# Four blocks of a 31-tap convolution get set places behind the heads' projections on VectorE's queue

## The chip, the cores and the metric

The kernel runs on one core of a Trainium2 chip. The metric is the device time of one execution in microseconds; the kernel before takes 781.31 us (median of three runs, 781.28 to 781.71). The core has five engines with queues of their own, each worked through in order: TensorE (PE in the profile; its weight loads are listed as PEld), VectorE (DVE), ScalarE (ACT), GpSimd (POOL) and SyncE (SP), which issues most of the loads. An engine waits at the head of its queue until what its next instruction needs is there.

## What is computed

One layer of a decoder, for 512 positions of 1024 channels. A first half mixes two groups of channels that come from one input projection: four mLSTM heads of 256 channels, and a convolution group. A second half is a feed-forward network with a short convolution. Both are scaled by a modulation that a second input c gives. Cut to what the change touches:

```python
u = rms_norm(x, mix_pre_g) * (1.0 + sc1) + sh1
proj = u @ w_in
qk_raw, v, o_pre, gates, glu = jnp.split(proj, [2*D_ML, 3*D_ML, 4*D_ML, 4*D_ML + 2*H], axis=-1)

qk = jax.nn.silu(causal_dwconv(qk_raw, qk_conv_w, qk_conv_b))      # 4 taps
h = mlstm_chunkwise(q, k, v, igates, fgates)                       # 4 heads
h = rms_norm(h) * jax.nn.sigmoid(o_pre)

a, gt = jnp.split(glu, 2, axis=-1)
y = causal_dwconv(a * jax.nn.sigmoid(gt), cv_dw_w, cv_dw_b)        # 31 taps
y = jax.nn.silu(layer_norm(y, cv_ln_g, cv_ln_b))

mix = jnp.concatenate([h, y], axis=-1) @ w_out
x = x + g1 * rms_norm(mix, mix_post_g)
```

## The kernel before

Channels lie on the 128 partitions and the 512 positions along the free dimension, so the 1024 channels of the convolution group are eight tiles of 128 x 512, the blocks 0 to 7. Products on TensorE are made of three parts: each operand is split into a rounded high part (`hi`, a copy on ScalarE) and the rest (`lo`, a subtraction, mostly on GpSimd), and `mm3` (L186 to L190) adds high x high, high x low and low x high in one PSUM bank. The weights come through two raw buffers, loaded from SyncE's queue, and are split in `w_split` (L164).

The order of the stages on TensorE is: the projection of the convolution group (`glu`), v of head 0, then for each head six projections of 128 channels (two of q, two of k, two of the output gate o), its attention, and v of the next head; then the output projection, in which the convolution's result y is used as well, and the feed-forward half. `head_proj(h, i)` (L430) makes projection i of head h: 24 matmuls, and for q and k (`i < 4`) the short convolution `conv4` (L408): a start on ScalarE (L412), three taps on VectorE (L414) and a Silu on ScalarE (L415). `attention(h)` (L447) is a generator: its pieces are called between the projections of the next head (L705 to L731). At its end VectorE scales the head's rows (`hn`, L482) by a factor that GpSimd computes (L477 to L479), TensorE turns them (`hT`, L488), and VectorE and ScalarE gate and split them (L490 to L494). `make_E` (L531) makes the next head's decay factors: a product `Mb` (L533), a masked copy `Md` on VectorE (L535), and exponentials on ScalarE (L540, L542).

The long convolution is the loop at L646 over the eight blocks. In a block, ScalarE writes the first term into a PSUM bank (`cp`, L649; there are two such banks), ScalarE and GpSimd make five further taps in SBUF (L655, L657; the tiles of the pool `cvs`, four of them), and VectorE adds the other 25 taps, one instruction each, all into the same bank (L661): tap d covers 512 - d positions, so a block's taps run from 506 columns down to 482. Then ScalarE copies the bank out (L663), GpSimd adds the five side taps (L665), and running sums of the mean and the square over the blocks follow (L671 to L676). TensorE reads these sums in `norm_mean` (L682), late in the third turn of the head loop, and y is then normalised in `norm_rows` (L695).

SyncE and TensorE work in the order in which the code is written. The order on VectorE, ScalarE and GpSimd is made when the kernel is built, by a planner that goes through its own model of time and puts the ready instruction with the lowest priority number next on each engine's queue. The priority is a counter that rises with the code; work between `tc.cur_priority += LATER` and its reverse gets 100000 more, so the convolution's blocks fill the places that the heads' work leaves. An edge given by hand (`tc.add_manual_dep` with the class NoSync) tells the planner that one instruction must stand behind another on the same queue; it adds no wait on the chip.

Behind the last tap of the last block stand eight products of the modulation (`ada_block(i, last_tap)`, i from 16 to 23, L734): each is a load of 512 KB issued from ScalarE's queue (L153) into one of two buffers, and one instruction on VectorE (L155) with its accumulator read. Their result is needed for the first gains (L738).

Of the kernel before, what the change touches and what calls it, by code (L numbers as in the profile page):

```python
# [14 lines left out]
ALU = mybir.AluOpType  # L15
# [4 lines left out]
T = 512  # L20
KT = D // P
# [5 lines left out]
CK = 31  # L27
LATER = 100000
# [24 lines left out]
def decoder_layer(ctx, tc, w_glu0, x, c, adaT, vecs, w_glu, w_qko, w_v0, w_v, w_out, w_up, w_down, out):  # L53
    nc = tc.nc
    V, S, G, PE = nc.vector, nc.scalar, nc.gpsimd, nc.tensor
# [28 lines left out]
    def slot(name, dt=F32):  # L84
        return slots.tile([P, T], dt, tag="t", name=name)

    def mmbank(name):
        return psum.tile([P, T], F32, tag="mm", bufs=4, name=name)

    def atbank(name):  # L90
        return psum.tile([P, T], F32, tag="at", bufs=2, name=name)
# [5 lines left out]
    def cvbank(name):  # L97
        return cvpool[0].tile([P, T], F32, tag="cv", name=name)
# [30 lines left out]
    def vcol(name, i):  # L129
        a = VEC[name][0] + i  # L130
        return vec[:, a : a + 1]
# [15 lines left out]
    def ada_block(i, behind):  # L147

        if i % 6 < 4 and 24 <= i < 40:
            r = spare[0][:, 2 * (i % 6) : 2 * (i % 6) + 2, :].rearrange("p j t -> p (j t)")  # L150
        else:
            r = adas.tile([P, D], F32, tag="ada", name=f"ada_{i}")
        nc.scalar.dma_start(r, adaT[i // 2][:, (i % 2) * D : (i % 2 + 1) * D])  # L153
        junk = small.tile([P, D], BF16, tag="junk", bufs=1, name=f"junk_{i}")
        t = V.scalar_tensor_tensor(out=junk, in0=r, scalar=1.0, in1=cb, op0=ALU.mult, op1=ALU.mult, accum_out=mod[:, i : i + 1])  # L155
        tc.add_manual_dep(t.ins, behind.ins.name, mybir.DependencyInfo(mybir.DependencyClass.NoSync, mybir.DependencyReason.DATA),
                          reason="order on VectorE")

    def ada_done(a, b):
        V.tensor_tensor(out=mod[:, a:b], in0=mod[:, a:b], in1=vcols("ada_b", a, b - a), op=ALU.add)  # L160
# [84 lines left out]
    for tt in range(NT):  # L245
# [11 lines left out]
        if tt == NT - 1:  # L257
# [9 lines left out]
                    op0=ALU.add)  # L267
# [80 lines left out]
    cvx = [None] * KT  # L348
# [8 lines left out]
    def proj(ps, pieces, off):  # L357
        for k in range(KT):
            mm3(ps, blk(pieces, off + k), u[k], k == 0, k == KT - 1)
# [4 lines left out]
    for i in range(G0 // 2, KT):  # L364
        glu_weights(i)
        for half in range(2):
            ps = mmbank(f"glu{i}_{half}")
# [40 lines left out]
    def conv4(ps, i, name):  # L408

        t = slot(f"{name}c")  # L410
        w = lambda tap: vcol("qk_conv_w", tap * 16 + i)
        S.activation(t, ps, AF.Identity, bias=vcol("qk_conv_b", i), scale=w(3))  # L412
        for d in range(1, 4):
            V.scalar_tensor_tensor(out=t[:, d:], in0=ps[:, : T - d], scalar=w(3 - d), in1=t[:, d:], op0=ALU.mult, op1=ALU.add)  # L414
        S.activation(t, t, AF.Silu)  # L415
        return t

# [2 lines left out]
    hy = [None] * (2 * KT)  # L420

    heads = {}

    def head_load(h):
        pieces = []
        for part in range(3):
            pieces += w_load(w_qko[3 * h + part], f"wqko{h}_{part}")
        heads[h] = (pieces, [], [], [])

    def head_proj(h, i):  # L430

        pieces, qs, ks, so = heads[h]
        ps = mmbank(f"qko{h}_{i}")
        proj(ps, pieces, i * KT)
        e = 2 * h + i % 2
        if i < 2:
            qs.append(conv4(ps, e, f"q{h}_{i}"))
        elif i < 4:
            ks.append(conv4(ps, 8 + e, f"k{h}_{i}"))
        else:  # L440
            t = slot(f"so{h}_{i}")
            S.activation(t, ps, AF.Tanh, scale=0.5)
            so.append(t)

    last_lo = [None]

# [96 lines left out]
    head_load(0)  # L543
    for i in range(3):
        head_proj(0, i)

    fps = atbank("fcum")
    fv = fps[:, : NT * H].rearrange("p (t h) -> p t h", t=NT)
# [3 lines left out]
    V.tensor_copy(Fc, fv)  # L552
    V.tensor_tensor(out=ga, in0=gz[:, :, :H], in1=Fc, op=ALU.subtract)
    head_proj(0, 3)

    aps = atbank("aT")
# [5 lines left out]
    S.activation(Ms[:H, :], Mr, AF.Copy)  # L562
    V.tensor_tensor(out=Ms[LOW : LOW + H, :], in0=Mr, in1=Ms[:H, :].bitcast(F32), op=ALU.subtract)
    head_proj(0, 4)
    mps = atbank("mtok")
    mv = mps[:, : NT * H].rearrange("p (t h) -> p t h", t=NT)
# [38 lines left out]
    def cvtile(name):  # L605
        return cvs.tile([P, T], F32, tag="cvs", name=name)
# [31 lines left out]
            mm3(ps, (hy[k][0][:, tok(tt)], hy[k][1][:, tok(tt)]), wo[0][n % 4], n == 0, n == 2 * KT - 1)  # L638


    tc.cur_priority += LATER

    ys = [None] * KT
    ysum = const.tile([P, T], F32, name="ysum")
    ysq = const.tile([P, T], F32, name="ysq")
    for j in range(KT):  # L646
        cp = cvbank(f"cv{j}")
        w = lambda tap: cvw[:, tap * KT + j : tap * KT + j + 1]
        S.activation(cp, cvx[j], AF.Identity, bias=vcol("cv_dw_b", j), scale=w(CK - 1))  # L649
        side = None  # L650
        for d in range(1, SIDE + 1):
            t = cvs.tile([P, T], F32, tag="cvs", name=f"cs{j}_{d}")
            if d == 1:
                V.memset(t[:, :d], 0.0)
            S.activation(t[:, d:], cvx[j][:, : T - d], AF.Copy, scale=w(CK - 1 - d))  # L655
            if side is not None:
                G.tensor_tensor(out=side[:, d:], in0=side[:, d:], in1=t[:, d:], op=ALU.add)  # L657
            else:
                side = t
        for d in range(SIDE + 1, CK):  # L660
            last_tap = V.scalar_tensor_tensor(out=cp[:, d:], in0=cvx[j][:, : T - d], scalar=w(CK - 1 - d), in1=cp[:, d:], op0=ALU.mult, op1=ALU.add)  # L661
        y = cvx[j]
        S.activation(y, cp, AF.Copy)  # L663
        if side is not None:
            G.tensor_tensor(out=y, in0=y, in1=side, op=ALU.add)  # L665
        ys[j] = y

        if j:
            mean_of = ys[0] if j == 1 else ysum
            dl = cvtile(f"ydl{j}")  # L670
            V.scalar_tensor_tensor(out=dl, in0=mean_of, scalar=-1.0 / j, in1=y, op0=ALU.mult, op1=ALU.add)  # L671
            dst = ysq if j == 1 else dl
            S.activation(dst, dl, AF.Square, scale=(j / (j + 1.0)) ** 0.5)
            if j > 1:
                G.tensor_tensor(out=ysq, in0=ysq, in1=dl, op=ALU.add)
            G.tensor_tensor(out=ysum, in0=mean_of, in1=y, op=ALU.add)  # L676
    tc.cur_priority -= LATER

    def norm_mean():

# [51 lines left out]

    tc.cur_priority += LATER
    for i in range(16, 24):  # L734
        ada_block(i, last_tap)
    ada_done(16, 24)
    tc.cur_priority -= LATER
    gain(0, 16, "mix_post_g")  # L738
# [208 lines left out]
    for i in range(NF):  # L947
        if i < NE:
            pa, pg = early[i]
        else:  # L950
# [11 lines left out]
            for half in range(2):  # L962
                ps = mmbank(f"up{i}_{half}")
# [290 lines left out]
```

## Time and profile before

| what | value |
|---|---|
| median of three runs | 781.31 us |
| the profiled execution | 782.39 us |
| its span, first to last instruction | 780.6 us |
| granted TensorE clock, mean | 0.997 |
| busy: PE, DVE, ACT, POOL | 761.7, 591.3, 407.6, 383.9 us |
| convolution taps on VectorE (L661) | 200, 134.2 us, 54.4 to 232.6 us |
| the eight modulation products (L155) | 233.3 to 259.0 us |

Times are in microseconds from the start of the span. A row of the order of time gives the start, the duration, the engine, the line, the operation, the tiles (result <- operands) with their shapes, a count where rows of one kind are merged, and in square brackets the idle time of the engine before it and what ended it. ACTq is the issue of a transfer from ScalarE's queue. A row of the list of waits gives engine, tile and line that waited, what it waited for, the total time, the number of waits and the longest. The end of a matmul is modelled, and a busy TensorE is not one at its peak; its starts are what to go by.

### The profile page before, as it was taken

To read this page: it belongs to the slowest core of one execution; us is meant where nothing else is said; L and a number is where in the kernel's file an instruction comes from. 1 tells how busy PE (TensorE), PEld (TensorE's weight loads), DVE (VectorE), ACT (ScalarE), POOL (GpSimd) and SP (SyncE) were. 2 spreads that over 40 slices of the span, in tenths; PEclk is the share of its full clock that TensorE was granted. 3 is DMA by queue.
4 is the path that set the end of the run, shared out by engine and by line. 5 is a ranking of instruction groups with operands and counts; after the bars stand their busy time and mean duration, and the time that the engine had idled before them with its cause. 6 is when DMAs were issued, how large, how long until landed. Compare 5 with 4: busy or idle time off the path is not lost.

```text
span 780.6 us, 10572 instructions
## 1 busy us (share of the span) xinstructions
PE 761.7 (98%) x3683; PEld 635.0 (81%) x3683; DVE 591.3 (76%) x938; ACT 407.6 (52%) x766; POOL 383.9 (49%) x313
## 2 busy tenths in 40 slices
PE   7899999999999999999999999999999999999996
PEld 4678898878888888888878998888888888888884
DVE  7659999999998533555868799665556677699997
ACT  6576428668655554482244445444444444456762
POOL 3689759779778534334661446544454440000001
PEclk9999999999999999999999999999999999999998
DMA  8973313303117432424952763332333321777862
GB/s 297 325 293 126 107 58 108 135 29 109 55 57 248 154 103 86 143 105 144 391 196 103 242 230 136 129 108 93 124 115 128 116 101 61 260 273 235 299 241 108
DMA packets 35977, 124.28 MB, mean 159 GB/s; under 512 B 4146, under 2 KB 5586, under 8 KB 29908
## 3 DMA queue, kind: packets, MB, share of 16 engines
q1 hardware_dynamic: 24084, 95.15, 34.8%
q10 hardware_dynamic: 11840, 28.46, 10.2%
q8 instruction: 29, 0.48, 0.2%
q14 instruction: 24, 0.20, 0.1%
HBM read 112.17 MB, written 11.42 MB: 158 GB/s over the span
## 4 chain that ended last, share of the span: by engine, by line
PE 80%; DVE 10%; DMA 4%; issue 3%; POOL 1%; ACT 1%; ACTq 0%; POOLq 0%; DVEq 0%; SPq 0%
PE up L189 10%; PE up L188 10%; PE up L190 10%; DVE cv L661 5%; PE qko L188 4%; PE qko L189 4%; PE qko L190 4%; PE p L190 4%; PE p L189 4%; PE p L188 4%; PE glu L189 3%; PE glu L190 3%; PE glu L188 3%; DMA spare<-in_adaT 2%; PE o L466 2%
## 5 line engine op out<-in xcount | busy, mean ns | idle before, releaser
L661 DVE SCALAR_TENSOR_TENSOR cv<-gt,cvw,cv 128x506 f32<-128x506 f32 (+24 forms) x200 | 134.2, 728 | 0.4
L617 POOL TENSOR_TENSOR ro2r<-ro2t,mhalf 128x1 f32<-128x1 f32 x1 | 0.5, 538 | 120.7 <-DVE ro2t L615 120.7
L171 POOL TENSOR_TENSOR wup_1024l<-wup,wup_1024h 128x512 fp32r<-128x512 f32 x20 | 27.8, 1388 | 31.6 <-ACT wup_1024h L170 22.2
L171 POOL TENSOR_TENSOR wup_0l<-wup,wup_0h 128x512 fp32r<-128x512 f32 x20 | 27.8, 1388 | 29.4 <-ACT wup_0h L170 29.4
L657 POOL TENSOR_TENSOR cs<-cs,cs 128x510 f32<-128x510 f32 (+3 forms) x32 | 42.0, 1312 | 0.2
L171 POOL TENSOR_TENSOR wup_1536l<-wup,wup_1536h 128x512 fp32r<-128x512 f32 x20 | 28.4, 1422 | 27.2 <-ACT wup_1536h L170 27.2
L189 PE MATMUL up<-u2l,wup_0h 128*128 128x512 f32 (+1 forms) x100 | 36.5, 365 | 0.2 <-DVE u2l L830 0.2
L188 PE MATMUL up<-u2h,wup_0h 128*128 128x512 f32 (+1 forms) x100 | 36.5, 365 | 0.0
L188 PE MATMUL up<-u2h,wup_1024h 128*128 128x512 f32 (+1 forms) x100 | 36.4, 364 | 0.0
L190 PE MATMUL up<-u2h,wup_0l 128*128 128x512 f32 (+1 forms) x100 | 36.4, 364 | 0.0
L188 PE MATMUL up<-u2h,wup_512h 128*128 128x512 f32 (+1 forms) x100 | 36.4, 364 | 0.0
L189 PE MATMUL up<-u2l,wup_512h 128*128 128x512 f32 (+1 forms) x100 | 36.4, 364 | 0.0
L190 PE MATMUL up<-u2h,wup_512l 128*128 128x512 f32 (+1 forms) x100 | 36.4, 364 | 0.0
L188 PE MATMUL up<-u2h,wup_1536h 128*128 128x512 f32 (+1 forms) x100 | 36.4, 364 | 0.0
L189 PE MATMUL up<-u2l,wup_1536h 128*128 128x512 f32 (+1 forms) x100 | 36.4, 364 | 0.0
L190 PE MATMUL up<-u2h,wup_1536l 128*128 128x512 f32 (+1 forms) x100 | 36.4, 364 | 0.0
L190 PE MATMUL up<-u2h,wup_1024l 128*128 128x512 f32 (+1 forms) x100 | 36.4, 364 | 0.0
L189 PE MATMUL up<-u2l,wup_1024h 128*128 128x512 f32 (+1 forms) x100 | 36.3, 363 | 0.0
L155 DVE SCALAR_TENSOR_TENSOR junk<-ada,cb 128x1024 bf16<-128x1024 f32 x20 | 31.0, 1551 | 7.0 <-DMA ada<-in_adaT 6.7
L171 POOL TENSOR_TENSOR wup_512l<-wup,wup_512h 128x512 fp32r<-128x512 f32 x20 | 27.2, 1358 | 14.6 <-ACT wup_512h L170 14.6
L655 ACT ACTIVATE cs<-gt,cvw 128x511 f32<-128x511 f32 (+4 forms) x40 | 27.2, 712 | 5.0 <-POOL cs L657 4.1
L171 POOL TENSOR_TENSOR wqko_1024l<-wqko,wqko_1024h 128x512 fp32r<-128x512 f32 x12 | 16.6, 1380 | 21.9 <-PE v L189 12.3
(1061 smaller groups left out, 2680.6 us busy)
## 6 DMA issues: line engine op xcount, KB each, us to landing
wup<-in_w_up SPq DMA_DIRECT2D x22, 1024.0 KB, 8.3
wqko<-in_w_qko SPq DMA_DIRECT2D x12, 1024.0 KB, 5.0
ada<-in_adaT ACTq DMA_DIRECT2D x20, 512.0 KB, 5.9
ada<-in_adaT SPq DMA_DIRECT2D x16, 512.0 KB, 5.9
wo<-in_w_out SPq DMA_DIRECT2D x8, 1024.0 KB, 9.2
spare<-in_adaT ACTq DMA_DIRECT2D x12, 512.0 KB, 7.3
wglu<-in_w_glu SPq DMA_DIRECT2D x5, 1024.0 KB, 7.7
wd<-in_w_down SPq DMA_DIRECT2D x6, 768.0 KB
```

Source lines behind the costliest of these rows:

```text
L155: t = V.scalar_tensor_tensor(out=junk, in0=r, scalar=1.0, in1=cb, op0=ALU.mult, op1=ALU.mult, accum_out=mod[:, i : i + 1])
L171: (eng or G).tensor_tensor(out=lo[:, :n], in0=src, in1=hi[:, :n].bitcast(F32), op=ALU.subtract)
L188: PE.matmul(ps, a[0], b[0], start=start, stop=False)
L189: PE.matmul(ps, a[0], b[1], start=False, stop=False)
L190: PE.matmul(ps, a[1], b[0], start=False, stop=stop)
L466: PE.matmul(o[:, : DH + 2], E[h][cc][:, a : a + P], vs[h][cc], start=cc == 0, stop=cc == tt)
L617: G.tensor_tensor(out=r, in0=t, in1=mhalf[:, :1], op=ALU.pow)
L655: S.activation(t[:, d:], cvx[j][:, : T - d], AF.Copy, scale=w(CK - 1 - d))
L657: G.tensor_tensor(out=side[:, d:], in0=side[:, d:], in1=t[:, d:], op=ALU.add)
L661: last_tap = V.scalar_tensor_tensor(out=cp[:, d:], in0=cvx[j][:, : T - d], scalar=w(CK - 1 - d), in1=cp[:, d:], op0=ALU.mult, op1=ALU.add)
```

## The change

The body of the loop becomes a function `cv_block(j, behind)`. Blocks 0 to 4 are called where the loop stood; blocks 5, 6 and 7 are called from `head_proj`, after projection (head 1, 0), (head 1, 3) and (head 2, 1). Blocks 4 to 7 get an edge: the first of their 25 taps on VectorE must stand behind a set tap of the short convolutions, for block 4 the last tap of projection (head 0, 2), for the others the last tap of the projection that calls them. `conv4` keeps its last tap for this. Nothing else of a block is held by an edge, but the later call gives blocks 5 to 7 later priority numbers, still with the 100000 added. The eight modulation products stay behind the last tap of block 7. No instruction is added or taken away.

```diff
         for d in range(1, 4):
-            V.scalar_tensor_tensor(out=t[:, d:], in0=ps[:, : T - d], scalar=w(3 - d), in1=t[:, d:], op0=ALU.mult, op1=ALU.add)
+            last_conv4[0] = V.scalar_tensor_tensor(out=t[:, d:], in0=ps[:, : T - d], scalar=w(3 - d), in1=t[:, d:], op0=ALU.mult, op1=ALU.add)
...
+    last_conv4 = [None]
+
+    CV_BEHIND = {(1, 0): 5, (1, 3): 6, (2, 1): 7}
...
+        if (h, i) in CV_BEHIND:
+            cv_block(CV_BEHIND[h, i], last_conv4[0])
...
     for i in range(3):
         head_proj(0, i)
+    head0_tap = last_conv4[0]
...
-    for j in range(KT):
+    last_tap = [None]
+
+    def cv_block(j, behind=None):
+
+        tc.cur_priority += LATER
         cp = cvbank(f"cv{j}")
...
         for d in range(SIDE + 1, CK):
-            last_tap = V.scalar_tensor_tensor(out=cp[:, d:], in0=cvx[j][:, : T - d], scalar=w(CK - 1 - d), in1=cp[:, d:], op0=ALU.mult, op1=ALU.add)
+            last_tap[0] = V.scalar_tensor_tensor(out=cp[:, d:], in0=cvx[j][:, : T - d], scalar=w(CK - 1 - d), in1=cp[:, d:], op0=ALU.mult, op1=ALU.add)
+            if behind is not None:
+                tc.add_manual_dep(last_tap[0].ins, behind.ins.name, mybir.DependencyInfo(mybir.DependencyClass.NoSync, mybir.DependencyReason.DATA),
+                                  reason="order on VectorE")
+                behind = None
...
-    tc.cur_priority -= LATER
+        tc.cur_priority -= LATER
+
+    for j in range(5):
+        cv_block(j, head0_tap if j == 4 else None)
...
     for i in range(16, 24):
-        ada_block(i, last_tap)
+        ada_block(i, last_tap[0])
```

More of the change, by code (lines that the diff above doesn't have):

```diff
@@ L638, in mix_first @@
             mm3(ps, (hy[k][0][:, tok(tt)], hy[k][1][:, tok(tt)]), wo[0][n % 4], n == 0, n == 2 * KT - 1)
-    tc.cur_priority += LATER
     ys = [None] * KT
```

## The prediction

> **What bounds the kernel now.** I read the page first (span and busy times), then the list of what TensorE waited for between 127 and 310 us, then busy time by stretch, and last the order of time on VectorE around the taps that move.
>
> ```profile
> span 780.6 us, 10572 instructions
> ...
> PE 761.7 (98%) x3683; PEld 635.0 (81%) x3683; DVE 591.3 (76%) x938; ACT 407.6 (52%) x766; POOL 383.9 (49%) x313
> ```
> ```profile
> PE hT L488 <- DVE hn L482: 1.4, 1, 1.4
> PE hT L488 <- ACT E L542: 0.4, 1, 0.4
> ```
>
> TensorE is busy for 761.7 of 780.6 us, and its order is fixed by hand, so the end can move only by what TensorE waits for. From the first head's projections to the end of the heads, where all that the change moves lies, it waits twice: 1.4 us for VectorE's scaled head (hn), 0.4 us for ScalarE's factors E. The convolution's taps (8 blocks of 25) fill VectorE:
>
> ```profile
> 146.00:208.00 62.00, 61.17 (x303) 50.70 (x301) 61.94 (x100) 43.93 (x90) 50.41 (x42) 1.00 0.24 83
> 208.00:235.00 27.00, 26.47 (x128) 21.47 (x129) 26.68 (x46) 15.89 (x26) 19.70 (x15) 1.00 0.16 50
> 235.00:264.00 29.00, 28.66 (x163) 25.12 (x161) 20.64 (x32) 14.71 (x38) 21.15 (x15) 1.00 0.71 244
> ```
> ```profile
> 146.00:208.00 62.00, 44.28 (x66) 2.76 (x4) 1.00 0.24 83
> ```
>
> The first table gives for each stretch the length, then busy time of PE, PEld, DVE, ACT, POOL, granted clock, DMA share, GB/s; the second is the convolution's accumulator alone, VectorE then ScalarE. VectorE is full from 146 to 235 (61.94 of 62, 26.68 of 27) and has room after that; TensorE lacks under 1 us in the first stretch, half a microsecond in the second. The clock is 1.00 throughout and does not enter.
>
> **The change, part by part.**
>
> *The four holds.* Each hold names a tap of a head's short convolution behind which the block's first tap (506 columns) must stand. On VectorE they stand now:
>
> ```profile
> 127.17 0.74 DVE L661 SCALAR_TENSOR_TENSOR cv<-gt,cvw,cv 128x506 f32<-128x506 f32 x1
> ...
> 142.87 0.74 DVE L661 SCALAR_TENSOR_TENSOR cv<-gt,cvw,cv 128x506 f32<-128x506 f32 x1
> ...
> 145.47 0.73 DVE L414 SCALAR_TENSOR_TENSOR k_2c<-qko,vec,k_2c 128x509 f32<-128x509 f32 x1
> ...
> 171.48 0.74 DVE L414 SCALAR_TENSOR_TENSOR q_0c<-qko,vec,q_0c 128x509 f32<-128x509 f32 x1
> ...
> 177.77 1.38 DVE L661 SCALAR_TENSOR_TENSOR cv<-gt,cvw,cv 128x506 f32<-128x506 f32 x2
> ...
> 191.92 0.74 DVE L414 SCALAR_TENSOR_TENSOR k_3c<-qko,vec,k_3c 128x509 f32<-128x509 f32 x1
> ```
> ```profile
> 193.21 0.74 DVE L661 SCALAR_TENSOR_TENSOR cv<-gt,cvw,cv 128x506 f32<-128x506 f32 x1
> ```
> ```profile
> 234.87 0.74 DVE L414 SCALAR_TENSOR_TENSOR q_1c<-qko,vec,q_1c 128x509 f32<-128x509 f32 x1
> ```
>
> Block 4 goes from 127.17 to behind 145.47 (18 us later), block 5 from 142.87 to behind 171.48 (29), block 6 from 177.77 to behind 191.92 (14), block 7 from 193.21 to behind 234.87 (42). All four set points lie after the present place, so none is idle. The holds have no price in themselves: they order one queue, and nothing but the block's own chain need stand behind a held tap, since the planner fills the queue with whatever else is ready.
>
> *What replaces the taps.* From 146 to 208 the other VectorE work is 61.94 - 44.28 = 17.7 us, which leaves 44.3 us for taps. How many that is depends on how they follow one another:
>
> ```profile
> 54.37 3.88 DVE L661 SCALAR_TENSOR_TENSOR cv<-gt,cvw,cv 128x506 f32<-128x506 f32 x5
> ```
> ```profile
> 66.54 9.70 DVE L661 SCALAR_TENSOR_TENSOR cv<-gt,cvw,cv 128x501 f32<-128x501 f32 x15
> ```
>
> The five at 54.37 belong to one block, each adding to the last: 3.88 / 5 = 0.78 us each. The fifteen at 66.54 alternate between two blocks: 9.70 / 15 = 0.65 us. So a block on its own costs 0.13 us more per tap, unless something else stands between. The 44.3 us take 57 taps (alone) to 68 (in pairs), and blocks 4, 5 and 6 have 75 to give: VectorE stays full up to 208, with blocks 5 and 6 in the place of 6 and 7. From 208 to 235 some 7 to 18 taps are left where 24 stand now, so VectorE falls idle there for 4 to 14 us.
>
> *Block 7 behind 234.87.* It needs 25 x 0.65 = 16.2 to 25 x 0.78 = 19.5 us of VectorE. It ends about 257 to 264, as the modulation products that fill 235 to 264 today wait for its last tap and move back with it:
>
> ```profile
> L155 DVE SCALAR_TENSOR_TENSOR junk<-ada,cb x8: 1209/1572/2139, 233.3 to 257.8; 128x1024 bf16<-128x1024 f32 x8
> ```
> ```profile
> DMA to landing us min/median/max: 4.8/5.4/5.9
> ```
>
> Eight products of 1.57 us are 12.6 us, so the rest of that stretch is 20.64 - 12.6 = 8 us and 8 + 16.2 to 19.5 fit into 29. The eight products, each pair with a 5.4 us load through two buffers, then end near 290. The sum over channels that wants block 7 is read by TensorE at 309:
>
> ```profile
> 310.18 0.69 DVE L684 SCALAR_TENSOR_TENSOR ydm<-ytot,ysum 128x512 f32<-128x512 f32 x1 [0.17 <-PE ytot L682]
> ```
>
> That leaves 45 us of cover, and the gains of these products are sent later still: both are costed at nothing. ScalarE's start, five shifted copies, copy-out and square per block, and GpSimd's sums, are not held; they move with their block as filler and no TensorE wait listed hangs on them.
>
> *The wait at 208.* The end of head 0:
>
> ```profile
> 202.32 0.68 DVE L535 TENSOR_TENSOR Md<-Mb,cmask 128x512 f32<-128x512 f32 x1
> 202.92 5.21 DVE L661 SCALAR_TENSOR_TENSOR cv<-gt,cvw,cv 128x501 f32<-128x501 f32 x8
> 208.04 1.13 DVE L482 TENSOR_SCALAR hn<-hn,fac 128x256 f32<-128x256 f32 x4
> ```
> ```profile
> 204.55 1.05 POOL L479 TENSOR_TENSOR fac<-ssq,mhalf 128x4 f32<-128x4 f32 x1
> ```
> ```profile
> 206.89 0.28 PE L190 MATMUL v<-wv_5h,ul 128*128 128x256 f32 x1
> 208.53 0.76 PE L488 MATMUL hT<-ident,hn 128*128 128x128 f32 x3 [1.36 <-DVE hn L482]
> ```
>
> GpSimd's factor is there at 205.60, yet hn starts at 208.04, because eight taps of blocks 6 and 7 in turn stand ahead of it. TensorE follows hn by 0.49 us (208.04 to 208.53) and loses 1.36 us. With block 7 gone from this place its four taps go too: four taps of block 6, alone, take 4 x 0.78 = 3.1 us in place of 5.2, and hn can start at 206.0, TensorE at 206.5, before its last product for v ends. The wait goes: -1.36 us. The bounds are 0 (other taps of block 6 are put in their place) and -1.36. I take the full -1.36, because the four taps are the very ones the hold forbids here; the next thing late would be the factor itself, 0.4 us earlier than hn.
>
> *The wait at 264.* ScalarE's queue in head 1's end:
>
> ```profile
> 259.10 0.33 ACTq L153 DMA_DIRECT2D ada<-in_adaT  x1
> 259.48 0.63 ACT L170 ACTIVATE wqko_512h<-wqko 128x512 fp32r<-128x512 f32 x1 [3.86 <-DVE gains L599]
> ```
> ```profile
> 263.61 0.36 ACT L542 ACTIVATE E<-Mb,ga 128x128 f32<-128x128 f32 x1
> ```
> ```profile
> 259.39 0.68 DVE L535 TENSOR_TENSOR Md<-Mb,cmask 128x512 f32<-128x512 f32 x1
> ```
>
> ScalarE stands 3.86 us up to 259.48, behind a load of the modulation rows (the ACTq row) that waits for VectorE's product to free the buffer; the factors E end at 263.97 and TensorE's second transpose waits 0.36 us for their bank. With the eight products moved back, this load no longer stands here. Md, which stands behind two of those products up to 259.39, may now stand behind taps of block 7 instead; the 2.4 us that hn lost so at 208 are the size of that, and no more than it loses now (2 x 1.57). So -0.36 us; bounds: 0 (a load still stands ahead) and -0.6, the weight load's own wait for the same bank:
>
> ```profile
> PEld hT L488 <- ACT E L542: 0.6, 1, 0.6
> ```
> ```profile
> PEld aT L558 <- DVE ga L553: 0.4, 1, 0.4
> ```
>
> The second row is the only other weight load in this region that hangs on VectorE, at 143, where the hold of block 4 clears the queue; I count it for the bound alone.
>
> **Sum.** -1.36 - 0.36 = -1.7 us. The profiled execution took 782.39 us (span 780.6 and 1.8 around it), so it would become 780.7; it lies 1.08 us above the median of the runs, 781.31, and against that the forecast is 779.6.
>
> **Rivals.**
>
> *The gap is refilled* (no change to be measured). VectorE stays full to 208, as computed, and ready taps of block 6 can be placed ahead of hn just as eight were before. For it: 57 to 68 places for 75 taps. Against it: a lone block offers one tap at a time. Then only the wait at 264 goes: 780.9 to 781.3, chance 0.28. This is also how the hold could do what it says and be worth nothing.
>
> *The lone block runs late* (slower). Place: VectorE's queue from 146 to 208. If the order is planned as though a tap cost 0.65 us, 57 lone taps lag by up to 57 x 0.13 = 7.4 us, by half of that where every second tap has a neighbour. hn then comes at 208.04 - 2.1 + 3.7 to 7.4 = 209.6 to 213.3 in place of 208.04, and the 1.6 to 5.3 us fall on TensorE; less 0.36: 782.5 to 786.2. It decides when hn starts after 206.5. For it: hn already stands 2.4 us behind its factor. Against it: q_1c at 230 finds VectorE idle although block 7 ran alone there, as the next row says. Chance 0.20, middle 784.
>
> ```profile
> 230.68 0.75 DVE L414 SCALAR_TENSOR_TENSOR q_1c<-qko,vec,q_1c 128x511 f32<-128x511 f32 x1 [0.22 <-ACT q_1c L412]
> ```
>
> [...]
>
> *The loads land worse* (slower). The eight loads stay on ScalarE's queue, now from about 257 on. If one of them, waiting 3.86 us as above, stands ahead of the factors E, TensorE's wait at 264 grows from 0.36 to up to 4.2 us: 781.31 - 1.36 + 3.9 = 783.8. Chance 0.07. Another 0.05 goes to an order of the weight splits on ScalarE and GpSimd that leaves TensorE short elsewhere.
>
> **How the numbers follow.** A median of three runs tells about 0.2% (1.6 us) from no change, so faster is under 779.75 and slower over 782.87. Both waits go: 0.40, of it 0.28 under 779.75 (centre 779.6, own range 778.9 to 780.5) and 0.12 within. Refilled: 0.28, of it 0.02 faster. Lone block late: 0.20, of it 0.04 within. Loads 0.07 and elsewhere 0.05: slower. Together faster 0.30, same 0.42, slower 0.28. The range begins at 781.31 - 1.36 - 0.6 - 0.4 = 778.9 and reaches to 784.0, the middle of the late block, with little more than 1 in 10 beyond it.
>
> **What would show it.** Right: the wait of hT for hn near 207 is gone and hn starts by 206.5; taps of block 7 start after 234.9 and end by 264; the eight products end near 290; the idle of VectorE appears near 133 to 146 and 208 to 235. Wrong: a wait for hn of 1 us or more at 207 (refilled or late), of more than 0.4 us at 264 (loads), or a new wait of TensorE for a weight split.

## The result and the profile after

The changed kernel takes 779.87 us (median of 12 runs, 779.4 to 783.06), the kernel before on the same chip 781.83 us (12 runs, 781.28 to 782.42). The ratio is 0.998, with a 95% interval of 0.9971 to 0.9989: faster by 0.2%, some 1.6 us, and the interval leaves room for 0.9 to 2.3 us (the two medians lie 1.96 us apart). The forecast was 779.6 us.

The profiled execution took 780.55 us (span 778.8); that of before had 782.39 (span 780.6). First the list of what TensorE waited for after the change, all of it but the last row (engine, tile and line, what it waited for, total us, number, longest):

```profile
PE xT L232 <- DVE xn L237: 2.5, 3, 1.5
PE cps L139 <- DMA crow<-in_c: 2.2, 1, 2.2
PE glu L189 <- POOL ul L331: 2.0, 2, 1.6
PE glu L338 <- ACT uh L328: 0.5, 1, 0.5
PE s L460 <- DVE E L461: 0.5, 1, 0.5
```

The first four belong to the opening, which the change doesn't touch. Both waits of hT, on hn and on E, are gone. One row is new: half a microsecond of s for VectorE's E. A wait for the gains has also gone, which the list of before shows in this row:

```profile
PE gT L585 <- DVE gains L783: 1.2, 1, 1.2
```

A second profiled execution of the kernel before, below, doesn't have it, so it comes and goes without the change; whether the change makes it rarer isn't shown. Nor does it explain why the profiled execution of before lay above the median: the execution without it took 3 us longer, and against the median of all 12 runs, 781.83 us, the 1.08 us are only 0.56.

Busy time by stretch after the change (length, then PE, PEld, DVE, ACT, POOL, clock, DMA share, GB/s), and then the convolution's accumulator alone on VectorE and ScalarE:

```profile
146.00:208.00 62.00, 62.00 (x310) 51.86 (x310) 60.79 (x94) 39.41 (x82) 43.35 (x37) 1.00 0.23 82
208.00:235.00 27.00, 26.93 (x131) 21.85 (x129) 22.77 (x35) 19.82 (x34) 25.22 (x21) 1.00 0.14 42
235.00:264.00 29.00, 29.00 (x173) 25.87 (x171) 27.55 (x42) 15.76 (x41) 17.12 (x16) 1.00 0.38 135
```
```profile
146.00:208.00 62.00, 41.45 (x59) 2.75 (x4) 1.00 0.23 82
```

TensorE is now busy in all three stretches to within 0.07 us. VectorE does 59 taps from 146 to 208 where it did 66, and has its idle time (4.2 us) between 208 and 235. The end of head 0 on VectorE:

```profile
191.76 4.59 DVE L669 SCALAR_TENSOR_TENSOR cv<-gt,cvw,cv 128x506 f32<-128x506 f32 x7
196.26 0.16 DVE L395 COPY v<-ones 128x8 f32<-128x8 f32 x1
196.33 0.15 DVE L481 TENSOR_TENSOR dm<-dm,em 128x4 f32<-128x4 f32 x1
196.40 2.64 DVE L669 SCALAR_TENSOR_TENSOR cv<-gt,cvw,cv 128x486 f32<-128x486 f32 x4
198.96 2.46 DVE L487 TENSOR_SCALAR hn<-hn,fac 128x256 f32<-128x256 f32 x4
```

hn starts at 198.96, nine microseconds earlier than before (208.04), and not at the 206.0 that the prediction worked out from a factor at 205.60. So the factor itself has moved, by 7.45 us. Most of that is GpSimd's doing. Its order before:

```profile
196.63 1.29 POOL L657 TENSOR_TENSOR cs<-cs,cs 128x510 f32<-128x510 f32 x1
197.87 1.29 POOL L675 TENSOR_TENSOR ysq<-ysq,ydl 128x512 f32<-128x512 f32 x1
199.26 0.20 POOL L477 TENSOR_TENSOR dm<-dm 128x4 f32<-128x4 f32 x1
199.41 1.30 POOL L171 TENSOR_TENSOR wqko_0l<-wqko,wqko_0h 128x512 fp32r<-128x512 f32 x1
200.67 1.30 POOL L657 TENSOR_TENSOR cs<-cs,cs 128x509 f32<-128x509 f32 x1
201.91 0.22 POOL L478 TENSOR_TENSOR ssq<-ssq,dm 128x4 f32<-128x4 f32 x1
```

and after:

```profile
196.56 0.20 POOL L482 TENSOR_TENSOR dm<-dm 128x4 f32<-128x4 f32 x1 [2.17 <-DVE dm L481]
196.84 0.20 POOL L483 TENSOR_TENSOR ssq<-ssq,dm 128x4 f32<-128x4 f32 x1
197.12 1.03 POOL L484 TENSOR_TENSOR fac<-ssq,mhalf 128x4 f32<-128x4 f32 x1
...
207.16 1.29 POOL L677 TENSOR_TENSOR gt<-gt,cs 128x512 f32<-128x512 f32 x1 [6.41 <-ACT gt L675]
...
210.86 1.29 POOL L665 TENSOR_TENSOR cs<-cs,cs 128x510 f32<-128x510 f32 x1
```

Before, three small operations (dm, ssq, fac) stood between weight splits and the side sums of block 6 (cs, 1.3 us each), and took from 199.26 to 205.60. After, GpSimd had been idle for 2.17 us when dm came, did all three in a row, and was done at 198.15; the side sums of block 6 come only at 210.86. The three operations take 4.75 us less from first start to last end; the other 2.70 us are that dm comes to GpSimd sooner. ScalarE has the head's dm at 193.48 in place of 196.10, where three shifted copies of block 6 (194.26, 1.93 us) stood ahead of it, and VectorE has its own dm at 196.33 in place of 197.90, in 0.15 us in place of 1.28. What keeps the side sums away is the pool of four tiles that the side taps share with the mean update (ydl): in both traces so far the first write of a block's side taps (a memset) follows the mean update of the block before, at 194.51 and 195.24 before. Block 5's hold moves the end of its last tap from 191.4 to 205.2, and with it the mean update and the memset:

```profile
208.85 0.68 DVE L683 SCALAR_TENSOR_TENSOR ydl<-ysum,gt 128x512 f32<-128x512 f32 x1
209.46 0.73 DVE L669 SCALAR_TENSOR_TENSOR cv<-gt,cvw,cv 128x493 f32<-128x493 f32 x1
209.48 0.06 DVE L662 MEMSET cs<- 128x1 f32 x1
```

This gives two explanations for the wait at 208. **Theory A**, the prediction's: block 7's taps leave the queue ahead of hn. **Theory B**, from the trace: block 5's hold delays its mean update, GpSimd is free when the head needs it, and the factor comes 7.5 us earlier.

### The profile page after: what moved, and what is told of

It is laid out like the page before. It is cut to its first block, busy times and chain, and to the rows that moved or that the text cites. A ratio compares the mean times of both kernels' runs of the same rounds, so it can differ in the third digit from the quotient of the medians.

```text
span 778.8 us, 10571 instructions
## 1 busy us (share of the span) xinstructions
PE 762.8 (98%) x3683; PEld 636.8 (82%) x3683; DVE 598.5 (77%) x938; ACT 407.4 (52%) x766; POOL 381.7 (49%) x313
## 4 chain that ended last, share of the span: by engine, by line
PE 71%; DVE 17%; ACT 4%; DMA 4%; POOL 2%; issue 1%; SPq 0%; POOLq 0%; DVEq 0%; ACTq 0%
PE up L190 10%; PE up L189 10%; PE up L188 10%; DVE cv L669 8%; PE p L189 4%; PE p L190 4%; PE p L188 4%; PE glu L189 3%; PE glu L190 2%; PE glu L188 2%; DMA wglu<-in_w_glu 2%; PE mixa L188 2%; PE mixa L190 2%; PE mixa L189 2%; PE mixb L188 2%; PE mixb L190 2%
## 5 line engine op out<-in xcount | busy, mean ns | idle before, releaser
L669 DVE SCALAR_TENSOR_TENSOR cv<-gt,cvw,cv 128x506 f32<-128x506 f32 (+23 forms) x200 | 137.9, 730 | 1.8
L170 ACT ACTIVATE wup_1024h<-wup 128x512 fp32r<-128x512 f32 x22 | 13.9, 631 | 25.2 <-PE up L189 21.5
```

The lines of the kernel that those rows point to most:

```text
L170: S.activation(hi[:, :n], src, AF.Copy)
L669: last_tap[0] = V.scalar_tensor_tensor(out=cp[:, d:], in0=cvx[j][:, : T - d], scalar=w(CK - 1 - d), in1=cp[:, d:], op0=ALU.mult, op1=ALU.add)
```

## The experiments

Ratios are to the kernel before on the same chip, with 95% intervals. In the table of holds, `True` means that the block's first tap is held, `False` that the block is only called there; the call in `head_proj` goes through that list.

**Block 7 alone held.** Blocks 0 to 6 are called in the loop's place.

```diff
-    CV_BEHIND = {(1, 0): 5, (1, 3): 6, (2, 1): 7}
+    CV_BEHIND = {(2, 1): [(7, True)]}
...
-    for j in range(5):
-        cv_block(j, head0_tap if j == 4 else None)
+    for j in range(7):
+        cv_block(j, None)
```

> Only block 7 is held, behind the last tap of projection (head 2, 1); blocks 0 to 6 stand where they stood before. Theory A (the prediction: TensorE's wait for hn near 207 ends because block 7's taps leave VectorE's queue ahead of hn): hn starts by 206.5, GpSimd's factor still ends near 205.6, that wait of 1.4 us is gone, and as the modulation products move back the 0.4 us wait at 264 is gone too: 1.2 to 2 us faster than before. Theory B (the wait ends because GpSimd is free when the factor is due: the side sums of block 6 cannot start before the mean of block 5 is taken, and holding block 5 puts that after 206): here block 5 ends as before, the side sums of block 6 still stand between 195 and 206 on GpSimd, the factor ends at 205 or later, hn starts no earlier than 205.7, and a wait for hn of 0.3 us or more stays; only the wait at 264 surely goes: 0.4 to 1.5 us faster.

779.28 us, ratio 0.9973 (0.9962 to 0.9983). Nothing beyond the opening and one wait of 0.2 us is left on TensorE's list. The factor is as late as before, and VectorE does in kind what the prediction described: taps of block 6 alone stand ahead of hn, at 0.76 us each. They are six, not four, as Md already starts at 200.15 (202.32 before), and VectorE then even waits for the factor:

```profile
200.75 4.55 DVE L670 SCALAR_TENSOR_TENSOR cv<-gt,cvw,cv 128x490 f32<-128x490 f32 x6
205.61 2.15 DVE L488 TENSOR_SCALAR hn<-hn,fac 128x256 f32<-128x256 f32 x4 [0.31 <-POOL fac L485]
```

So Theory A's route exists, and the hold of block 7 alone gives all of the gain.

**Block 5 alone held**, blocks 6 and 7 called behind it without a hold.

```diff
-    CV_BEHIND = {(1, 0): 5, (1, 3): 6, (2, 1): 7}
+    CV_BEHIND = {(1, 0): [(5, True), (6, False), (7, False)]}
...
-        cv_block(j, head0_tap if j == 4 else None)
+        cv_block(j, None)
```

> Only block 5 is held, behind the last tap of projection (head 1, 0); 6 and 7 follow it without a hold. Theory A: taps of blocks 6 and 7 can stand ahead of hn as before, the wait for hn near 207 stays at 1 us or more, the one at 264 as well: within 0.5 us of before. Theory B: block 5's mean comes after 200, GpSimd has no side sums between 195 and 205, the factor ends by 200, hn starts by 201 and the wait near 207 is gone; the modulation products stay near 235 to 262 and so does the 0.4 us wait at 264: 1.0 to 1.6 us faster.

787.27 us, ratio 1.0073 (1.0061 to 1.0086): slower, which neither theory had forecast. The wait at 208 is gone (factor at 198.1, hn at 198.8), as Theory B has it. But two larger waits come at head 1's end, one new and one grown from 0.4:

```profile
PE s L461 <- DVE so L496: 4.2, 1, 4.2
...
PE hT L494 <- ACT E L548: 1.6, 1, 1.6
```
```profile
267.31 1.23 DVE L155 SCALAR_TENSOR_TENSOR junk<-ada,cb 128x1024 bf16<-128x1024 f32 x1 [3.02 <-DMA ada<-in_adaT]
...
269.92 1.23 DVE L155 SCALAR_TENSOR_TENSOR junk<-ada,cb 128x1024 bf16<-128x1024 f32 x1 [1.37 <-DMA ada<-in_adaT]
...
271.07 0.68 DVE L496 SCALAR_TENSOR_TENSOR so<-so,hT 128x512 f32<-128x512 f32 x1
```

Block 7 ends at 245 here, so the modulation products run from 245 to 271. VectorE stands 3.02 and 1.37 us for their loads, with the head's gate (so) queued behind them, and TensorE waits 4.24 us for the bank that so frees. The 1.6 us for E come another way: hn of head 1 waits for GpSimd's factor, and Md, which E needs, starts behind it at 261.21 (255.31 in the changed kernel):

```profile
259.12 2.17 DVE L488 TENSOR_SCALAR hn<-hn,fac 128x256 f32<-128x256 f32 x4 [2.60 <-POOL fac L485]
```

**All but block 5 held**: blocks 4, 6 and 7 as in the change, block 5 in the loop's place.

```diff
-    CV_BEHIND = {(1, 0): 5, (1, 3): 6, (2, 1): 7}
+    CV_BEHIND = {(1, 3): [(6, True)], (2, 1): [(7, True)]}
...
-    for j in range(5):
+    for j in range(6):
```

> As the change, but block 5 has no hold and stands in the loop's place; 4, 6 and 7 are held. Theory A: block 7 is still away from hn, the wait near 207 is gone: within 0.4 us of the changed kernel. Theory B: block 5 ends before 195, the side sums of block 6 are back between 195 and 206, the factor ends after 203, and hn waits for it: the wait near 207 is back in part, 0.3 to 1.4 us slower than the changed kernel.

781.16 us, ratio 0.9991 (0.9975 to 1.0008): not told apart from before. Half of the wait at 208 is back:

```profile
PE hT L494 <- DVE hn L488: 0.7, 1, 0.7
```
```profile
203.86 3.82 DVE L670 SCALAR_TENSOR_TENSOR cv<-gt,cvw,cv 128x497 f32<-128x497 f32 x5
207.59 1.69 DVE L488 TENSOR_SCALAR hn<-hn,fac 128x256 f32<-128x256 f32 x3
```

The side sums of block 6 stand on GpSimd from 197.0 again, the factor comes at 205.99, and five lone taps of block 6 stand ahead of hn. With the changed kernel (0 us of wait, factor at 198.15) this says that there it is block 5's hold that ends the wait; with block 7 away but block 5 in its old place, the gap is partly refilled. Since block 7 alone held has no such wait, the holds of blocks 4 and 6 have a part in the refilling.

**Block 7 not held**: blocks 4, 5 and 6 as in the change, block 7 called right behind block 6.

```diff
-    CV_BEHIND = {(1, 0): 5, (1, 3): 6, (2, 1): 7}
+    CV_BEHIND = {(1, 0): [(5, True)], (1, 3): [(6, True), (7, False)]}
```

> As the change, but block 7 follows block 6 without a hold; 4, 5 and 6 are held. Theory A: taps of block 7 stand ahead of hn again, the wait near 207 is back with 1 us or more: 1 to 1.5 us slower than the changed kernel. Theory B: the wait near 207 stays away (factor by 200), block 7 ends 10 to 20 us earlier than in the changed kernel, so the modulation products come near 240 to 265; whether TensorE waits at 264 for E (before) or at 275 for its bank (changed kernel) follows from where they fall: within 0.6 us of the changed kernel.

788.22 us, ratio 1.0097 (1.0083 to 1.0111). The wait at 208 is gone without any hold on block 7 (factor at 197.7, hn at 198.5), so Theory B alone ends it. The price, again forecast by neither theory, is the same as with block 5 alone: products from 248 to 274, waits of 3.05 and 1.36 us for loads ahead of so, a late Md (261.86), and these waits of TensorE:

```profile
PE s L461 <- DVE so L496: 4.7, 2, 4.3
...
PE hT L494 <- ACT E L548: 2.1, 1, 2.1
```

**The kernel before, once more.**

> The kernel before, profiled once more. The wait of 1.2 us for the gains at 400, long after the last block, was in its first profile and is in none of the five changed ones. If it belongs to the kernel, it is here again with about 1 us; if it was that execution's luck with the loads, it is under 0.4 us. The waits of 1.4 us near 207 and 0.4 us at 264 belong to the order of the queues and are here again in either case.

One execution, 785.36 us, with these rows in its list:

```profile
PE hT L488 <- ACT E L542: 3.2, 1, 3.2
...
PE hT L488 <- DVE hn L482: 1.4, 1, 1.4
```

The 1.4 us for hn are the kernel's own. The wait for E is 3.2 us in place of 0.4, and what sets it is when one load lands:

```profile
260.77 1.22 DVE L155 SCALAR_TENSOR_TENSOR junk<-ada,cb 128x1024 bf16<-128x1024 f32 x1 [3.51 <-DMA ada<-in_adaT]
```
```profile
262.42 0.63 ACT L170 ACTIVATE wqko_512h<-wqko 128x512 fp32r<-128x512 f32 x1 [5.11 <-DVE gains L599]
```

This product ran at 257.85 in the first profile, without a wait. A load that lands some 3 us later goes through VectorE's queue and ScalarE's to TensorE, at 2.9 us (3.2 in place of 0.36). The wait for the gains isn't there. Of the 67 other timed executions of the kernel before, three took over 786 us and the rest at most 783.22, so the 0.4 us of the first profile is likely nearer to the usual size of this wait than the 3.2; what the three waited for isn't known.

**The products alone moved.** No block is held, all eight are called in the loop's place as before, and the eight products stand behind the last tap of head 3's first projection (`taps` keeps the last tap of each projection).

```diff
-        ada_block(i, last_tap[0])
+        ada_block(i, taps[3, 0])
```

> The kernel before with one edit: the eight modulation products stand behind the last tap of projection (head 3, 0), near 284, in place of the last tap of block 7; no block is held. If the 0.4 us wait at 264 came from their loads on ScalarE's queue, it is gone, and the wait for hn near 207 stays at 1 to 1.5 us: 0.3 to 0.7 us faster than before. If the holds are needed for the wait at 264 too, it stays and nothing is gained.

781.01 us, ratio 0.9988 (0.9973 to 1.0002). The wait for E is gone and the 1.4 us for hn stay. The two waits of before have two separate causes.

**Block 7 not held, products moved too.** The same two edits together.

> Blocks 4, 5 and 6 held, block 7 not (this was 6.9 us slower than before), and the eight modulation products behind the last tap of projection (head 3, 0). If those 6.9 us came from VectorE standing at a product whose load is late, ahead of the head's work, then the waits of 2.1 us at 262 and 4.3 us at 268 go and the time falls to 779.0 to 780.5. If they came from block 7's taps at 207 to 248, it stays above 785.

779.68 us, ratio 0.9978 (0.9965 to 0.9991), where block 7 unheld alone had 1.0097. Only 0.5 us of s for so is left, at head 0's end. So the taps of block 7 cost nothing in that place; what cost 1.2% was the products that follow its last tap.

**The changed kernel, products moved.**

> The changed kernel with the eight modulation products behind the last tap of projection (head 3, 0). The new wait of 0.5 us at 275 (attention's product waiting for the bank that E's update frees, behind two of the products) goes: 0.4 to 0.7 us faster than the changed kernel, 778.8 to 779.6, about the same as holding block 7 alone. If the products get into the way of the norm's work at 309 instead, a wait for ytot's successors or for the turns at 318 appears and the gain is lost.

779.0 us (778.67 to 779.58), ratio 0.9966 (0.9954 to 0.9979), and no wait is left between the opening and the feed-forward half. It is the lowest median of all, though its interval overlaps that of the change itself.

**The mean update with a buffer of its own.** The kernel before, no hold; the weight pool gives one of its 20 buffers for the room.

```diff
-            dl = cvtile(f"ydl{j}")
+            dl = cvs.tile([P, T], F32, tag="cvd", bufs=1, name=f"ydl{j}")
```

> The kernel before, no hold at all; the mean update's tile (ydl) gets a buffer of its own instead of one of the four that the side sums use (the weight pool gives up one of its 20 buffers for the room). Theory B (GpSimd's side sums of block 6, which start only after block 5's mean update because of the shared buffers, delay the head's factor): the side sums no longer wait for the mean update, GpSimd has them behind it when the factor comes, the factor is there before 201 in place of 205.6, hn starts before 206.5 and the 1.36 us wait at 207 goes although all of block 7's taps stay where they are: about 1.3 us faster than before, 780.0, unless the missing weight buffer costs something. Theory A (block 7's taps themselves are what holds hn): they stay in the queue, the wait of 1.36 us stays, same as before within 0.1%. Both: the wait at 264 stays (0.4 to 3 us).

785.18 us, ratio 1.0044 (1.003 to 1.0058). One part of Theory B is shown: the memset of a block's side taps no longer follows the mean update of the block before (block 6's memset at 153.9 with block 5's update at 197.1, block 7's at 174.2 with block 6's update at 231.6), so it was the shared buffers that tied them:

```profile
153.94 0.06 DVE L654 MEMSET cs<- 128x1 f32 x1
...
197.10 1.12 DVE L671 SCALAR_TENSOR_TENSOR ydl<-ysum,gt 128x512 f32<-128x512 f32 x1
```

The numbers expected were missed, since another order arose; how much of it comes from the missing weight buffer wasn't tried by itself. TensorE lost 3.3 us much earlier, near 147, for the gates (ga), which now stood behind more taps:

```profile
PE aT L558 <- DVE ga L553: 3.3, 1, 3.3
```

That put TensorE's last product for v at 212.35 in place of 206.89. The factor came at 205.95, late in time but 6.4 us ahead of that product where it had been 1.3 us ahead, and the wait for hn is gone. The wait for E, expected to stay, is gone too, and the one for the gains is there with 2.0 us. With TensorE itself late, this run can't say what the early factor alone is worth.

**The change and block 7 alone, side by side.** Both once more on one chip.

> The changed kernel once more, for a comparison on the same chip: ratio to before 0.997 to 0.999 again; the wait of 0.5 us at 275 for the factors' product there or not as the loads land.

> Only block 7 held, blocks 4 to 6 in the loop's place, on the same chip as the changed kernel. If the holds of blocks 4 to 6 are worth nothing, the same as the changed kernel within 0.1%; if they cost the 0.5 us wait at 275 and the opening's 0.9 us, 0.1 to 0.2% faster than it; if they are needed, slower than it.

779.96 us, ratio 0.9981 (0.9972 to 0.999), and 779.61 us, ratio 0.9971 (0.9958 to 0.9983). The change has the 0.5 us wait of s again, block 7 alone doesn't. The 0.35 us between the medians are less than the intervals tell apart. The profiles tell more: from its first projection product (qko) to its product for the norm's sums (ytot) TensorE needs 187.53 and 187.52 us in the two profiles of the change, and 186.84 in both of block 7 alone. So with block 7 held the holds of blocks 4 to 6 are of no use, and in the profiles they cost 0.7 us, of it the 0.5 us wait.

**Block 7 alone, products moved.**

> Only block 7 held, and the eight modulation products behind the last tap of head 3's first projection (as in the best version so far). No wait of TensorE between 150 and 310 is left in either version, so 0.3 to 0.4% faster than before, within 0.1% of the changed kernel with the same move (779.0); if the holds of blocks 4 to 6 cost something by themselves, up to 0.1% faster than that.

779.53 us, ratio 0.9986 (0.996 to 1.0012). Its seven runs reach from 778.72 to 786.36, so the interval says nothing (the other six end at 779.81); the profile has no wait between the opening and the feed-forward half.

## Why the prediction was right, point by point

**The sum.** Forecast -1.7 us, measured -1.6 (interval 0.9 to 2.3). In the profiles the waits in the heads come to -1.36 - 0.36 + 0.48 = -1.24 us; by TensorE's own starts, from the first qko to ytot, the heads take 187.53 us in place of 188.98, 1.45 less. That the total came so close to the forecast is in part luck: one term was right in size by another route, one was sized on an execution that can be far larger, and a cost of 0.48 us was put at nothing. Against the median of 12 runs, 781.83 us, the same sum gives 780.1.

**The wait at 208: size right, reason wrong for this kernel.** The step that failed is "GpSimd's factor is there at 205.60" taken as fixed: the side sums were said to "move with their block as filler", with no wait of TensorE hanging on them. In the changed kernel the factor came at 198.15, and block 7's hold isn't needed for it (block 7 unheld: gone as well). The wait at 208 did hang on them here, by way of the factor. The prediction's route is real, too: block 7 alone held gave hn at 205.61, six lone taps at 0.76 us ahead of it. The rival "the gap is refilled" is what all but block 5 held shows, with half its price (0.7 us).

**The wait at 264: right.** No load stands ahead of E any more, and Md comes at 255.31. The products moved alone show that these products were the cause. How large the term is depends on when one load lands: 0.36 us in the execution on which it was sized, 3.2 in the other.

**The products: cover right, end wrong.** They were to end near 290; they ran from 258.1 to 280.5, as block 7 ended at the early side of its range (258.1). Costed at nothing, they now cost half a microsecond at head 1's scores, as VectorE's E stands behind one of them:

```profile
273.72 0.68 DVE L461 SCALAR_TENSOR_TENSOR E<-s,E 128x512 f32<-128x512 f32 x1
274.32 1.21 DVE L155 SCALAR_TENSOR_TENSOR junk<-ada,cb 128x1024 bf16<-128x1024 f32 x1
...
275.46 0.55 DVE L461 SCALAR_TENSOR_TENSOR E<-s,E 128x384 f32<-128x384 f32 x1
```
```profile
276.06 0.49 PE L460 MATMUL s<-q_0c,k_2c 128*128 128x128 f32 x2 [0.48 <-DVE E L461]
```

The rival "the loads land worse" had this danger in mind, but on ScalarE's queue and ahead of E at 264. With block 5 alone held or block 7 unheld it came in full, on VectorE's queue and mostly at s (4.2 of 5.8 us and 4.7 of 6.8 us, not 3.9). In the changed kernel block 7 ends 13 and 10 us later than in these two; that this is what spares it is read from the order, not tried by itself.

**VectorE's fill: right.** 59 taps up to 208 (57 to 68 were worked out), 4.2 us of idle time from 208 to 235 (4 to 14). Block 7's first tap came at 233.33, 1.5 us before the time set, because its set point, the last tap of q_1c, itself moved up: its three taps now run without others between them (2.32 us from 231.09).

**The lone block: its price right, its damage absent.** A lone tap costs 0.77 us, as this row of block 4 has it (3.09 / 4), but VectorE had places enough (1.2 us idle up to 208), and no head operation came late for it:

```profile
143.53 3.09 DVE L669 SCALAR_TENSOR_TENSOR cv<-gt,cvw,cv 128x506 f32<-128x506 f32 x4
```

## What to carry to other kernels

A hold on one engine's queue also moves what the held work feeds on other engines: here a later mean update on VectorE kept its buffer, and so took 1.3 us sums out of GpSimd's queue just where a head needed three small operations. When a planner fills places, look at every instruction that shares a buffer with the moved work, not at the moved queue alone. And an instruction that waits for a transfer on an in-order queue costs that transfer's lateness to all behind it: put such products where nothing urgent follows, by an edge of their own rather than behind filler whose end drifts. And count a long wait of TensorE for more than its length, as the next section shows.

## What the runs showed of the hardware

A tiny operation on VectorE can cost as much as a large one on GpSimd beside it. The same 128x4 product dm took 0.15 us after the change and 1.28 before:

```profile
197.90 1.28 DVE L476 TENSOR_TENSOR dm<-dm,em 128x4 f32<-128x4 f32 x1
```

It started 0.03 us behind GpSimd's ysq (197.87 for 1.29 us, quoted above) and ended with it, within 0.02 us. The trace agrees here with the Trainium skill, page "SBUF — State Buffer", section "Who interferes with whom": a VectorE instruction with two inputs in SBUF contends with a GpSimd one that reads SBUF, and the port pair that they share is an exclusive lock. The modulation products show the same size of effect: 1.2 us alone, 2.32 beside a weight split on GpSimd that itself takes 2.27 in place of 1.3:

```profile
269.79 2.32 DVE L155 SCALAR_TENSOR_TENSOR junk<-ada,cb 128x1024 bf16<-128x1024 f32 x1
```
```profile
270.98 2.27 POOL L171 TENSOR_TENSOR wqko_512l<-wqko,wqko_512h 128x512 fp32r<-128x512 f32 x1
```

Both rows are of the changed kernel. An unexpected size was also the spread between two executions of the kernel before, 782.39 and 785.36 us: 2.9 us of wait came with one late load, while the 1.2 us for the gains went. The other 1.3 us come with a lower clock. Behind the wait of 3.22 us the profile has a granted clock of 0.86 from 264 to 268 and 0.71 from 268 to 272, where the first profile has 1.00, and products for v start 0.21 us apart in place of 0.12. From the first qko to ytot TensorE takes 4.31 us longer (193.29 in place of 188.98), 1.45 more than the wait grew.

The same stands behind the other single waits of over 3 us: 0.66 from 148 to 152 in the run with a buffer of its own for the mean update (3.3 us), 0.58 and 0.63 from 272 to 276 with block 5 alone held and with block 7 unheld (4.24 and 4.26 us). Behind the waits of 1.4 to 2.1 us in the heads of these runs the clock stayed at 1.00. Where between 2.1 and 3.2 us this sets in, and why, no run here shows.
